# Output projection of both layers as seven block products, with the sums of its weight blocks made by adding transfers

## The chip, the cores and the metric

One NeuronCore of one Trainium2 chip runs the whole program. The metric is the device time of one execution in microseconds (us). The engines have short names in the profile: PE (TensorE, matrix products), DVE (VectorE), ACT (ScalarE), POOL (GpSimd), SP (SyncE, which here only issues transfers). PEld is the loading of weights into PE.

## What is computed

A decoder of two layers over 1024 tokens of 1024 features, all in float32. The lines that matter here:

```python
o_a = dilated_mixture(...)            # window attention, three groups of heads
o_b = stick_breaking_attention(...)   # the "stick attention"
gates = sigmoid(gate_pre + b_gate[l])
g_a, g_b = gates[..., :D_MODEL], gates[..., D_MODEL:]
merged = g_a * (o_a @ w_br[l, :OUT_A]) + g_b * (o_b @ w_br[l, OUT_A:])
x = x + merged @ w_o[l]               # the output projection
h2 = rmsnorm(x, norm2[l])
up = h2 @ w_up[l]
a, v = up[..., :D_FF], up[..., D_FF:]
a = causal_depthwise_conv(a, conv_w[l], conv_b[l])
x = x + (gelu(a) * v) @ w_down[l]
```

The change concerns `merged @ w_o`, a product of two 1024 x 1024 matrices, once in each layer, and what stands just before and behind it.

## The kernel before

**Arithmetic.** Every float32 operand of a product is split in two: a high part (rounded by ACT with a copy) and a low part (the rest, by a DVE subtraction); `split` does both. One product of a 128x128 weight tile with 512 tokens is then three matmuls: high x high, high x low, low x high. Features lie on partitions, tokens on columns; the 1024 tokens are two halves `n` of 512, the 1024 features eight chunks `e` of 128.

**Order.** The program is written as Python generators that are stepped in turn. The order of PE's instructions is the written order. The other engines' orders come from a scheduler that uses priorities, except in the part of the feed-forward behind its second unit, where they are also the written order. Each engine runs its instructions strictly in its order: one that waits holds all behind it.

**A layer, in order.** (1) The input projection runs in the background of the attention: the class `Dense` hands PE pieces of it (`share` counts them) between the pieces of the stick attention, then of the window attention. In the stick attention POOL masks the diagonal block of every score tile (`affine_select` on `beta`). (2) The branch stage: sixteen pairs `(n, e)` in the order of `todo`. For each pair PE makes two products `br_ps` (one for each branch), DVE multiplies each with its gate (`gin`, the gates being loaded three pairs ahead and put through a sigmoid by ACT), DVE adds both (`mrg`), ACT makes the high part `hh` and POOL the low part `hl` by a subtraction. All eight accumulator banks are used in turn. (3) The output projection: `wo_chunk` for each half `n` and chunk `e` of output features loads the 1024 x 128 weights, splits them in two pieces (ACT and DVE), accumulates 8 x 3 matmuls in `o_ps`; DVE adds the result to the residual `x`; ACT squares it and DVE sums the squares for the norm. That is 16 chunks of 24 matmuls in each layer. (4) The norm of half 0 runs beside the second half of the projection, the norm of half 1 beside the first products of the feed-forward. (5) The feed-forward: two plain units (`u_ps`, up_plain), then twenty units `up(j)` of seven block products each (`u_a`, `u_c`, `u_b`), which need sums of blocks of the normed input. Four of these sums (`S[3]`) are made in `first_sum`, under the output projection, the others in `sums`, under the two plain units. In the units `up(j)` POOL already issues one adding transfer each: `up_a` += `up_a` within on-chip memory.

**Lines that the steps touch.** `split` 141, `weights` 160, `product` 177, `drive` 189, `first_sum` 531, `norm` 540, `seven` 1049, `wo_chunk` 1316, `merged` 1417, the loop of the branch stage 1433 to 1466, the end of `mixer` 1467 to 1477, `sums` 1628, `up` 1643.

Of the kernel before, what the change touches and what calls it, by code (L numbers as in the profile page):

```python
# [32 lines left out]
NRAW = 2  # L33
PT = 6
# [25 lines left out]
def f32(ap):  # L60
    return ap.bitcast(F32)
# [3 lines left out]
def trunk_kernel(ctx, tc, x, xt, head0, norm1, vecs, w_in, w_br, w_o, w_up, w_down, norm_f, out, depth=None, probe=None):  # L65
# [59 lines left out]
    dn = [dr.tile([4, T], F32, name=f"dn{i}") for i in range(2)]  # L125
    fd = dr.tile([4, T], F32, name="fd")
# [31 lines left out]


# [62 lines left out]
    class Dense:  # L222
# [4 lines left out]
        def __init__(self):  # L227
            self.main, self.plain, self.seven, self.done = [], [], [], set()
            self.side, self.later, self.hooks = [], {}, []
            self.now = self.nxt = None  # L230
# [252 lines left out]
    def norm_add(n, e, first=False):  # L483

        if first:
            ACC[n] = sb.tile([P, HF], F32, tag="ql", bufs=2, name="nrm")
# [829 lines left out]
    def wo_chunk(l, n, e):  # L1316
        w = weights(w_o[l][:, e * P : (e + 1) * P], P)
        yield
        o = bank("ps", "o_ps")
        yield from product(o, [(w[k], h_part(n, k)) for k in range(KD)])  # L1320
        dve.tensor_tensor(xc(n, e), xc(n, e), o, ALU.add)
        norm_add(n, e, e == 0)
        yield

    def mixer(l, pending):
        R.clear()
        dense = Dense()
        gates = [pair_gate(dense, l, e) for e in range(KD)]
# [36 lines left out]
        attend(dense, items)  # L1365
        oh = {}
# [49 lines left out]

        def merged(n, e, m):
            act.copy(H[n][0][:, e, :], m)
            pool.tensor_tensor(H[n][1][:, e, :], m, f32(H[n][0][:, e, :]), ALU.subtract)

        wo = [wo_chunk(l, n, e) for n in range(2) for e in range(KD)]
# [14 lines left out]
        for i, ab in order:  # L1436
            n, e = todo[i]
            sl = slice(n * HF, (n + 1) * HF)
            if i not in seen:
# [4 lines left out]
                if i in X_AT:  # L1444
                    late_x = X_AT.index(i)
                    x_in(l, late_x // 2, late_x % 2)
# [11 lines left out]
            m = small("mrg")  # L1458
            dve.tensor_tensor(m, gt[:, 0, :], gt[:, 1, :], ALU.add)
            late.append((n, e, m))  # L1460
# [5 lines left out]
            if i == 12:  # L1466
                next(wo[0])
# [4 lines left out]
        def first_half():  # L1472
            yield from norm(0, g2[:, 0, :], "t", keep=True)
            yield from first_sum()

        drive(first_half(), relay(*wo, primed=True), 2.5, 36)
        return norm(1, g2[:, 0, :], "t", AF.Gelu, True)

    def ffn(l, pending, final):
# [125 lines left out]
        def up_plain(j, order, turns, extra):  # L1605
# [3 lines left out]
            w = [up_weights(j, 0), up_weights(j, 1)]  # L1609
# [18 lines left out]
        def sums():  # L1628

            new_s(1)  # L1630
# [713 lines left out]
```

## Time and profile before

| | |
|---|---|
| median of the runs | 2591.91 us (2591.76 to 2598.05, 3 runs) |
| the profiled execution's own time | 2593.59 us |
| its span | 2591.8 us |
| PE busy | 2577.4 us, 12536 instructions |
| DVE busy | 2061.1 us |
| ACT busy | 1334.1 us |
| POOL busy | 130.0 us |
| granted clock of PE | 1.00 |

The profile is one execution. "Busy" is the time in which an engine works on an instruction; matmuls overlap, so a busy PE can still be a PE that takes longer between two matmuls than it has to. A row of a group gives line, engine, operation, names (out<-in), shapes, count, then busy time and mean duration of one, then the idle time just before them and what ended it. A row of the timeline gives start, duration, engine, line, names and, in brackets, the idle time before it and its releaser. A row of windows gives for a stretch of time each engine's busy time (and its instructions), PE's granted clock, the busy share of the 16 transfer engines and GB/s.

### The profile page before, as it was taken

The numbers are of one execution on the slowest core, as the hardware profiler recorded it, in microseconds if no ns is written. First come the engines' busy times: TensorE is split into PE (matmuls) and PEld (weight loads), VectorE is DVE, ScalarE is ACT, GpSimd is POOL, SyncE is SP. The second block draws the span as 40 slices with busy tenths as digits, with TensorE's granted clock in tenths as the row PEclk, the third lists the DMA queues.
The fourth block names the chain that finished last, engine by engine and source line by source line (L and its number), as shares of the span: only waits on it lengthen the run. The fifth ranks groups of instructions, "written<-read, shape, count | busy, mean of one in ns | idle before, by whom it ended". The sixth has DMA issues, their size and how long they took to land.

```text
span 2591.8 us, 35872 instructions
## 1 busy us (share of the span) xinstructions
PE 2577.4 (99%) x12536; PEld 2153.4 (83%) x12536; DVE 2061.1 (80%) x3410; ACT 1334.1 (51%) x2488; POOL 130.0 (5%) x175
## 2 busy tenths in 40 slices
PE   9999999999999999999999999999999999999999
PEld 8888888888888888888888888888888888888887
DVE  8878877796878878897677788778868888879966
ACT  6555566664554545432445555666645555544223
POOL 1000000030000000000000000000300000000000
PEclk9999999999999999999999999999999999999999
DMA  7434579863355455688344436798634455457963
GB/s 261 152 114 145 158 197 233 235 224 105 103 158 166 155 186 155 246 323 312 147 149 147 127 129 188 199 242 235 198 99 129 138 174 164 157 184 251 347 241 134
DMA packets 402579, 480.02 MB, mean 185 GB/s; under 512 B 25272, under 2 KB 311392, under 8 KB 400736
## 3 DMA queue, kind: packets, MB, share of 16 engines
q1 hardware_dynamic: 395776, 464.85, 56.0%
q0 software_dynamic: 6464, 12.62, 2.7%
q8 instruction: 99, 1.62, 0.3%
q14 instruction: 80, 0.66, 0.1%
q10 hardware_dynamic: 160, 0.27, 0.0%
HBM read 308.74 MB, written 158.43 MB: 180 GB/s over the span
## 4 chain that ended last, share of the span: by engine, by line
PE 92%; DVE 4%; ACT 2%; DMA 1%; issue 1%; POOL 0%; DVEq 0%; ACTq 0%; POOLq 0%
PE u_a L1053 5%; PE u_a L1052 5%; PE u_a L1054 5%; PE d_ps L1801 5%; PE d_ps L1802 5%; PE d_ps L1803 5%; PE i_a L1052 5%; PE i_a L1053 5%; PE i_a L1054 5%; PE u_c L1052 3%; PE u_c L1053 3%; PE u_c L1054 3%; PE i_c L1052 2%; PE i_c L1054 2%; PE i_c L1053 2%; PE o_ps L182 2%
## 5 line engine op out<-in xcount | busy, mean ns | idle before, releaser
L144 ACT CAST w_hi<-up_a 128x512 fp32r<-128x512 f32 x280 | 174.4, 624 | 265.1 <-DVE up_a L1658 133.4
L152 DVE TENSOR_TENSOR w_lo<-up_a,w_hi 128x512 fp32r<-128x512 f32 x280 | 189.4, 688 | 64.4 <-ACT w_hi L144 64.2
L144 ACT CAST w_hi<-in_a 128x512 fp32r<-128x512 f32 x252 | 156.2, 622 | 157.7 <-PE i_c L1053 33.6
L152 DVE TENSOR_TENSOR w_lo<-in_a,w_hi 128x512 fp32r<-128x512 f32 x252 | 173.1, 689 | 72.3 <-ACT w_hi L144 60.7
L1812 DVE TENSOR_TENSOR x<-x,d_ps 128x512 f32<-128x512 f32 x220 | 150.5, 685 | 59.5 <-PE d_ps L1803 56.3
L1052 PE MATMUL u_a<-hh,w_hi 128*128 128x512 f32 x320 | 124.5, 389 | 0.0
L1053 PE MATMUL u_a<-hl,w_hi 128*128 128x512 f32 x320 | 124.5, 389 | 0.0
L1054 PE MATMUL u_a<-hh,w_lo 128*128 128x512 f32 x320 | 124.5, 389 | 0.0
L1052 PE MATMUL u_a<-t_hi,w_hi 128*128 128x512 f32 x320 | 124.5, 389 | 0.0
L1053 PE MATMUL u_a<-t_lo,w_hi 128*128 128x512 f32 x320 | 124.5, 389 | 0.0
L1054 PE MATMUL u_a<-t_hi,w_lo 128*128 128x512 f32 x320 | 124.5, 389 | 0.0
L1801 PE MATMUL d_ps<-gd_in,w_hi 128*128 128x512 f32 x316 | 123.2, 390 | 0.0
L1802 PE MATMUL d_ps<-gd_in,w_hi 128*128 128x512 f32 x316 | 123.0, 389 | 0.0
L1803 PE MATMUL d_ps<-gd_in,w_lo 128*128 128x512 f32 x316 | 123.0, 389 | 0.0
L1052 PE MATMUL i_a<-hh,w_hi 128*128 128x512 f32 x288 | 117.8, 409 | 0.0
L1052 PE MATMUL i_a<-t_hi,w_hi 128*128 128x512 f32 x288 | 116.4, 404 | 0.0
L1054 PE MATMUL i_a<-t_hi,w_lo 128*128 128x512 f32 x288 | 113.0, 392 | 0.0
L1054 PE MATMUL i_a<-hh,w_lo 128*128 128x512 f32 x288 | 113.0, 392 | 0.0
L1053 PE MATMUL i_a<-hl,w_hi 128*128 128x512 f32 x288 | 112.9, 392 | 0.0
L1053 PE MATMUL i_a<-t_lo,w_hi 128*128 128x512 f32 x288 | 112.9, 392 | 0.0
L1801 PE MATMUL d_ps<-gd_in,wd 128*128 128x512 f32 x284 | 110.8, 390 | 0.0
L1803 PE MATMUL d_ps<-gd_in,wd 128*128 128x512 f32 x284 | 110.5, 389 | 0.0
(422 smaller groups left out, 7695.3 us busy)
## 6 DMA issues: line engine op xcount, KB each, us to landing
gd<-g SPq DMA_DIRECT2D x154, 512.0 KB, 3.4
gd_in<-gd SPq DMA_DIRECT2D x154, 512.0 KB, 6.2
up_a<-in_w_up_dram SPq DMA_DIRECT2D x80, 512.0 KB, 5.4
in_a<-in_w_in_dram SPq DMA_DIRECT2D x72, 512.0 KB, 5.4
wd_raw<-in_w_down_dram SPq DMA_DIRECT2D x22, 1024.0 KB, 9.5
gin<-gs SPq DMA_DIRECT2D x32, 512.0 KB, 4.5
w_raw<-in_w_o_dram SPq DMA_DIRECT2D x64, 256.0 KB, 2.9
gs<-u SPq DMA_DIRECT2D x48, 256.0 KB, 3.2
```

The lines of the kernel that those rows point to most:

```text
L144: one = act.copy(hi, src)
L152: two = dve.tensor_tensor(lo, src, f32(hi), ALU.subtract)
L182: pe.matmul(o, lh, rh, start=(first and i == 0), stop=False, skip_group_check=share)
L1052: pe.matmul(o, w[0][:, c], rh, start=(first and i == 0), stop=False, skip_group_check=True)
L1053: pe.matmul(o, w[0][:, c], rl, start=False, stop=False, skip_group_check=True)
L1054: pe.matmul(o, w[1][:, c], rh, start=False, stop=(last and i == 3), skip_group_check=True)
L1801: pe.matmul(o, wh[:, c], gh, start=(i == 0 and k in (0, 4, 5)), stop=False, skip_group_check=True)
L1802: pe.matmul(o, wh[:, c], gl, start=False, stop=False, skip_group_check=True)
L1803: pe.matmul(o, wl[:, c], gh, start=False, stop=(i == m - 1), skip_group_check=True)
L1812: dve.tensor_tensor(x, x, o, ALU.add)
```

## The change

The merged matrix and the weights are cut into 2 x 2 blocks: the weights by output half `f` and by even and odd chunks of 128 input features (`j`), the merged matrix by token half `n` and the same even and odd chunks. `out_proj` makes the product from seven block products (order 0, 4, 1, 2, 3, 5, 6), each of 4 output chunks x 4 input chunks x 3 matmuls, 336 in a layer where there were 384. That needs four sums of weight blocks and sums of blocks of the merged matrix.

- **Sums of weight blocks**: `prepare` runs in the stick attention, one step with each `share` behind the fourteenth: SP copies 16 blocks of the weights (256 KB each) to `wof` in the chip's main memory, then POOL issues 16 adding transfers into `wof`, one in four steps.
- **Splitting in the stage**: `out_proj` loads each product's weights and splits them one product ahead. For products 1 to 4 ACT and DVE do it as before; for products 0, 5 and 6 (`ADDING`) ACT makes the high part and its negative, and an adding transfer of POOL from main memory makes the low part of that (`split_on`).
- **Sums of the merged matrix**: `merge` keeps blocks of it in float32 (`keep`), with signs changed for some (a scalar-tensor operation in place of the addition); `added` makes the sums, some by DVE, some by adding transfers; `merged` splits the sums that are needed at once. Four of the sixteen POOL subtractions of a layer go to DVE. The sums of products 1 to 3 are split inside `out_proj` (`beside`).
- **Result**: products 0 to 3 accumulate in the same four banks, 5 and 6 in the same four; after each product DVE adds or subtracts each bank to or from `x`: 28 times in a layer where it was 16.
- **Around it**: loads of `x` come later (one in the branch stage, three in `out_proj`); the weights of the first feed-forward unit are loaded and split in `out_proj`; `first_sum` is gone from under the projection, its four sums are made in `sums`; the steps of the norms are placed differently, and `drive` at the start of the feed-forward takes 0.5 in place of 0.7 and 3 steps ahead in place of 2.

```diff
+PREP = 14
+GAP_SUM = 4
+ADDING = (0, 5, 6)
+ADD1 = 3
+LATER = 3
...
+    def split_on(hi, lo, raw, src):
+        act.copy(hi, raw)
+        act.mul(lo, f32(hi), -1.0)
+        nc.gpsimd.dma_start(lo, src.bitcast(F32R), accum_op=ALU.add)
...
             self.fetch()
+            if self.prep and self.count > PREP:
+                next(self.prep, None)
             return True
...
-    def wo_chunk(l, n, e):
-        w = weights(w_o[l][:, e * P : (e + 1) * P], P)
-        yield
-        o = bank("ps", "o_ps")
-        yield from product(o, [(w[k], h_part(n, k)) for k in range(KD)])
-        dve.tensor_tensor(xc(n, e), xc(n, e), o, ALU.add)
-        norm_add(n, e, e == 0)
-        yield
+    def prepare(l):
+        def behind(one):
+            tc.add_manual_dep(one.ins, LAST["hi"], NO_SYNC, reason="behind")
+        blocks = [blocks_of(l, i) for i in range(4)]
+        for s in range(4):
+            for i in range(4):
+                behind(nc.sync.dma_start(wof[s, i], blocks[i][(2, 0, 0, 1)[s]]))
+                yield
+        for s in (0, 2, 1, 3):
+            for i in range(4):
+                src = wof[1 if s == 3 else 0, i] if s % 2 else blocks[i][3 if s == 0 else 2]
+                how = dict(max_dma_last_dim=4 * HF) if s % 2 else {}
+                behind(nc.gpsimd.dma_start(wof[s, i], src, accum_op=ALU.add, **how))
+                for _ in range(GAP_SUM):
+                    yield
+
+    def out_proj(l, keep, added):
+        order = (0, 4, 1, 2, 3, 5, 6)
+        into = ((0, 0), (1, 0), (1, 1), (0, 1), (0, 0), (1, 1), (1, 0))
...
+        def two(k, *some):
+            if k not in ws:
+                ws[k] = place(k)
+            for i in some:
+                if k in ADDING:
+                    split_on(*ws[k][i], raws[k][i], source(k)[:, i, :])
+                else:
+                    split(*ws[k][i], raws[k][i])
...
+        def beside(k, e):
+            c11, c12, c21 = keep[0, 0], keep[1, 0], keep[0, 1]
+            def one(i):
+                hi, lo = sums[1][i]
+                act.mul(hi, c11[:, i, :], -1.0)
+                dve.scalar_tensor_tensor(lo, c11[:, i, :], -1.0, f32(hi), ALU.mult, ALU.subtract)
+            if k == 0:
+                if e == 0:
+                    new_sum(1)
+                two(4, e)
+                if e % 2:
+                    load(1, e // 2)
+                if e < 3:
+                    one(e)
+                if e == 1:
+                    added(0, 0, 3)
...
+            elif k == 4:
+                if e == 0:
+                    one(3)
+                    new_sum(2)
+                two(1, e)
+                split(*sums[2][e], c12[:, e, :])
...
+        for at, k in enumerate(order):
+            if k == 0:
+                banks[0] = banks[1] = banks[2] = banks[3] = [bank("to"[e // 2], "o_ps") for e in range(4)]
+            elif k in (4, 5):
+                banks[k] = banks[6] = [bank(("ps", "s")[e // 2], "o_ps") for e in range(4)]
+            for e in range(4):
+                o, c = banks[k][e], slice(e * P, (e + 1) * P)
+                for i in range(4):
+                    (wh, wl), (gh, gl) = ws[k][i], part(k, i)
+                    pe.matmul(o, wh[:, c], gh, start=(i == 0 and k in (0, 4, 5)), stop=False, skip_group_check=True)
+                    pe.matmul(o, wh[:, c], gl, start=False, stop=False, skip_group_check=True)
+                    pe.matmul(o, wl[:, c], gh, start=False, stop=(i == 3), skip_group_check=True)
+                    if i == 1:
+                        yield
+                n, f = into[k]
+                x = xc(n, 4 * f + e)
+                with tc.high_priority(offset=AHEAD):
+                    dve.tensor_tensor(x, x, o, ALU.add if f or k == 4 else ALU.subtract)
+                beside(k, e)
+                yield
...
+        def added(n, j, p):
+            if j == 0:
+                c = keep[0, 0][:, p, :]
+                dve.tensor_tensor(c, c, keep[1, 0][:, p, :], ALU.add)
+            else:
+                nc.gpsimd.dma_start(keep[0, 1][:, p, :], keep[0, 0][:, p, :], accum_op=ALU.add)
...
         def merged(n, e, m):
-            act.copy(H[n][0][:, e, :], m)
-            pool.tensor_tensor(H[n][1][:, e, :], m, f32(H[n][0][:, e, :]), ALU.subtract)
+            hi, lo = H[n][0][:, e, :], H[n][1][:, e, :]
+            if n and e % 2 == 0:
+                t = small("mrg")
+                dve.tensor_tensor(t, m, keep[0, 0][:, e // 2, :], ALU.add)
+                split(hi, lo, t)
+                return
+            act.copy(hi, m)
+            pool.tensor_tensor(lo, m, f32(hi), ALU.subtract)
+            if n:
+                nc.gpsimd.dma_start(keep[1, 0][:, e // 2, :], m, accum_op=ALU.add)
...
+            if i % 4 == ADD1 and i > 4:
+                added(0, 0, i // 4 - 1)
+            if i % 4 == 0 and i > 4:
+                added(0, 1, i // 4 - 2)
+            if i == 10:
+                wo = out_proj(l, keep, added)
+            if i in (10, 12, 14):
+                next(wo)
...
-        drive(first_half(), relay(*wo, primed=True), 2.5, 36)
+        side = norm(0, g2[:, 0, :], "t", keep=True)
+        for n in (43, 0, 0, 1, 1):
+            for _ in range(n):
+                next(wo)
+            next(side)
+        drive(side, wo, 1.0)
+        early["lead"] = LATER
...
         def sums():
+            new_s(3)
             new_s(1)
             new_s(2)
             for i in range(4):
                 b11, b12, b21, b22 = B[1, i], B[0, i], B[1, 4 + i], B[0, 4 + i]
+                s3 = small("s3")
+                dve.tensor_tensor(s3, b22, b12, ALU.subtract)
+                split(*S[3][i], s3)
```

**How it moves instructions.** On DVE, at the seam from the branch stage to the output projection of the first layer. Names: `gin` the last gate products, `mrg` a merged chunk, `w_lo` and `wo_in` low parts of weights, `x` the residual, `m_part` the kept blocks, `m_hi` and `m_lo` their two parts. Before, from the last `gin` on:

```order
L1454 TENSOR_TENSOR gin<-gin,br_ps 128x512 [waits PE_49,Activation_49]
L1459 TENSOR_TENSOR mrg<-gin 128x512 [waits DVE_49,Pool_49]
L152 TENSOR_TENSOR w_lo<-w_raw,w_hi 128x512 [waits DMAHW1_49,PE_49,Activation_49]
L1321 TENSOR_TENSOR x_5858<-x_5858,o_ps 128x512 [waits PE_49]
L152 TENSOR_TENSOR w_lo<-w_raw,w_hi 128x512 [waits DMAHW2_49,Activation_49]
```

Now, from the same `gin` to the fourth split of the second product's weights:

```order
L1656 TENSOR_TENSOR gin<-gin,br_ps 128x512 [waits PE_49]
L158 TENSOR_TENSOR wo_in<-wo_raw,wo_in 128x512 [waits Activation_49]
L1602 SCALAR_TENSOR_TENSOR mrg<-gin 128x512 [waits DVE_49]
L1618 TENSOR_TENSOR mrg<-m_part 128x512
L1491 TENSOR_TENSOR x_5971<-x_5971,o_ps 128x512 [waits PE_49]
L1411 SCALAR_TENSOR_TENSOR m_lo<-m_part,m_hi 128x512 [waits Activation_49]
L158 TENSOR_TENSOR hl_5829<-mrg,hh_5828 128x512 [waits Activation_49]
L158 TENSOR_TENSOR wo_in<-wo_raw,wo_in 128x512 [waits DMAHW5_49]
L1411 SCALAR_TENSOR_TENSOR m_lo<-m_part,m_hi 128x512
L1491 TENSOR_TENSOR x_5971<-x_5971,o_ps 128x512 [waits PE_49]
L1610 TENSOR_TENSOR m_part<-m_part 128x512 [waits DMASW7_49,Pool_49]
L158 TENSOR_TENSOR wo_in<-wo_raw,wo_in 128x512
```

Eleven rows now stand behind the last gate product up to the last weights that the second block product needs; one of them waits for an adding transfer (DMASW). From the first gate product of the stage to the last there are 63 rows, before 56.

On DVE, in the first layer, where the two plain feed-forward units end and `up(2)` begins. Names: `up_a` its weights, `cv` the convolution's tiles, `u_ps` the plain units' accumulators. Before:

```order
L152 TENSOR_TENSOR w_lo<-up_a,w_hi 128x512 [waits DMAHW4_49,PE_49]
L1521 SCALAR_TENSOR_TENSOR cv<-u_ps,vec,cv 128x511 [waits Activation_49]
L1526 SCALAR_TENSOR_TENSOR cv<-halo,vec,cv 128x1
L1522 SCALAR_TENSOR_TENSOR cv<-u_ps,vec,cv 128x510 [waits DVE_49]
L1527 SCALAR_TENSOR_TENSOR cv<-halo,vec,cv 128x2 [waits DVE_49]
L152 TENSOR_TENSOR w_lo<-up_a,w_hi 128x512 [waits DMAHW5_49,DMASW5_49,PE_49]
```

Now:

```order
L1742 TENSOR_TENSOR cv<-cv,u_ps 128x512 [waits PE_49,Activation_49]
L158 TENSOR_TENSOR t_lo<-b_f_6769,t_hi 128x512 [waits Activation_49]
L1852 TENSOR_TENSOR b_f_6815<-b_f_6972,b_f_6769 128x512
L158 TENSOR_TENSOR g<-cv,g 128x512 [waits DMAHW0_49,Activation_49]
L158 TENSOR_TENSOR w_lo<-up_a,w_hi 128x512 [waits DMAHW2_49]
L158 TENSOR_TENSOR w_lo<-up_a,w_hi 128x512 [waits DMAHW3_49,DMASW1_49]
```

The first low part of `up(2)`'s weights stood ahead of the instruction that waits for the last plain product (`cv<-cv,u_ps`); now it stands four rows behind the start of that one.

More of the change, by code (lines that the diff above doesn't have):

```diff
@@ L1457, in mixer @@
                 continue
[L1458 to L1460 removed]
+            late.append(merge(i, gt))
             if len(late) > 1:
```

113 lines of the change are left out of this document (99 added, 14 removed).

## The prediction

> **What bounds the kernel now.** I read the page first: which engine is busy, and which work forms the chain that ended last.
>
> ```profile
> span 2591.8 us, 35872 instructions
> PE 2577.4 (99%) x12536; PEld 2153.4 (83%) x12536; DVE 2061.1 (80%) x3410; ACT 1334.1 (51%) x2488; POOL 130.0 (5%) x175
> DVE  8878877796878878897677788778868888879966
> PE 92%; DVE 4%; ACT 2%; DMA 1%; issue 1%; POOL 0%; DVEq 0%; ACTq 0%; POOLq 0%
> ```
>
> PE is the bound: nearly all of the span and of the chain. A matmul that goes is time that goes, unless another engine is then late. DVE is the candidate: it stands at eight tenths or more in most slices. So next PE's timeline, for the pace of its matmuls and its waits at both ends of the stage that is changed.
>
> ```profile
> 570.21 0.39 PE L182 MATMUL o_ps<-hh,w_hi 128*128 128x512 f32 x1
> 574.74 0.39 PE L184 MATMUL o_ps<-hh,w_lo 128*128 128x512 f32 x1
> 575.91 0.50 PE L183 MATMUL o_ps<-hl,w_hi 128*128 128x512 f32 x1 [0.55 <-POOL hl L1419]
> 623.21 0.95 PE L546 MATMUL nrm_t<-ones,nrm 128*128 128x1 f32 x8
> 624.02 0.49 PE L182 MATMUL o_ps<-hh,w_hi 128*128 128x512 f32 x1
> 713.97 0.50 PE L1052 MATMUL u_c<-hh,w_hi 128*128 128x512 f32 x1 [0.57 <-ACT u L1674]
> 1998.15 0.50 PE L1052 MATMUL u_c<-hh,w_hi 128*128 128x512 f32 x1 [0.99 <-ACT u L1674]
> ```
>
> The first row is the first matmul of the output projection; the second comes 20 matmuls later, so the pace is 4.53/20 = 0.2265 us. Last I read the windows of three stages in both layers: first to last gate product (`gin`), the output projection, and the two plain feed-forward units.
>
> ```profile
> core 0: us, PE busy (x) PEld busy (x) DVE busy (x) ACT busy (x) POOL busy (x), PEclk, DMA share, GB/s
> 531.27:577.59 46.32, 45.77 (x202) 37.60 (x201) 43.83 (x57) 31.77 (x53) 19.81 (x15) 1.00 0.70 228
> 570.21:659.99 89.78, 89.04 (x397) 73.20 (x396) 59.09 (x88) 38.52 (x65) 5.32 (x5) 1.00 0.32 93
> 659.99:705.08 45.09, 45.09 (x206) 37.24 (x204) 43.07 (x75) 24.93 (x42) 1.80 (x2) 1.00 0.38 105
> 1816.00:1861.35 45.35, 45.35 (x202) 37.55 (x201) 43.43 (x57) 31.86 (x53) 20.33 (x15) 1.00 0.70 233
> 1854.94:1943.76 88.82, 88.75 (x398) 73.28 (x397) 58.26 (x87) 38.16 (x64) 5.18 (x4) 1.00 0.31 91
> 1943.76:1988.84 45.08, 45.08 (x205) 37.24 (x204) 42.38 (x74) 25.01 (x42) 1.78 (x2) 1.00 0.37 104
> ```
>
> The output projection has room on every other engine (DVE 59.09 of 89.78), but its neighbours have none on DVE: 43.83 of 46.32 and 43.07 of 45.09. The clock is full throughout. 384 matmuls take 86.98 by the pace; the first layer's 2.80 above that are about 1.2 for the norm's small products (0.81 from `nrm_t` to the next matmul, the rest an estimate for its broadcast) and 1.6 of waiting, the second layer's 1.84 the same 1.2 and 0.6.
>
> **The change part by part.** *Matmuls removed.* 48 in each layer, 96 x 0.2265 = **-21.7 us**, all on PE's path.
>
> *The seam into the output projection.* DVE finishes the gate products behind PE: PE starts the projection at 570.21 and 1854.94, DVE ends the last `gin` at 577.59 and 1861.35 (the windows' ends). What DVE has to do there, by these groups and rows:
>
> ```profile
> L1454 DVE TENSOR_TENSOR gin<-gin,br_ps 128x512 f32<-128x512 f32 x64 | 41.8, 679 | 2.0 <-ACT gin L1399 2.0
> L1459 DVE TENSOR_TENSOR mrg<-gin 128x512 f32<-128x512 f32 x32 | 32.6, 1018 | 2.4
> L152 DVE TENSOR_TENSOR br_w<-br_raw,br_w 128x512 fp32r<-128x512 f32 x16 | 13.0, 815 | 0.1
> L152 DVE TENSOR_TENSOR w_lo<-w_raw,w_hi 128x512 fp32r<-128x512 f32 x80 | 61.4, 771 | 35.4 <-ACT w_hi L144 35.1
> L152 DVE TENSOR_TENSOR g<-cv,g 128x512 fp32r<-128x512 f32 x154 | 105.7, 687 | 1.4 <-ACT g L144 1.4
> L1419 POOL TENSOR_TENSOR hl<-mrg,hh 128x512 fp32r<-128x512 f32 x32 | 44.4, 1392 | 170.3 <-ACT hh L1418 105.9 <-PE br_ps L184 64.4
> 705.35 0.69 DVE L1534 TENSOR_TENSOR cv<-cv,u_ps 128x512 f32<-128x512 f32 x1 [0.20 <-PE u_ps L184]
> 705.95 0.68 DVE L152 TENSOR_TENSOR w_lo<-up_a,w_hi 128x512 fp32r<-128x512 f32 x1
> ```
>
> The last two rows start 0.60 apart, though each lasts 0.69: a row of DVE costs 0.60. A POOL subtraction costs DVE too: the groups that run beside it are longer than the 687 of a plain subtraction, by 331 (`mrg`), 128 (`br_w`) and 84 (`w_raw`); (331x32 + 128x16 + 84x80)/32 = 0.60 us for each of the 32. From first to last `gin` there are now 63 DVE rows for 56: +4.2; four POOL subtractions fewer in each layer: -2.4. The last `gin` moves by +1.8, to 579.4 and 1863.15. Then eleven rows stand before the fourth split of the second product's weights, as the first pair of orders above shows: 6.6, and 1.2 for two POOL subtractions still running, so 587.2 and 1870.95. PE wants that low part 59 matmuls after its start (48 of the first product, 11 of the second): 583.6 and 1868.3. It waits 3.6 and 2.6.
>
> One of the eleven rows waits for an adding transfer, and so do three like it in the stage.
>
> ```profile
> L1651 POOL DMA_DIRECT2D up_a<-up_a x40 | 35.1, 878 | 905.1 <-DVE up_a L1661 235.3 <-DVE up_a L1658 180.0 <-DVE hl L566 178.7
> L723 POOL TENSOR_SCALAR_AFFINE_SELECT beta<-beta 128x128 f32<-128x128 f32 x64 | 31.4, 490 | 530.7 <-ACT beta L717 449.6 <-DMA in_a<-in_w_in_dram 42.0 <-DVE w_lo L152 28.8
> up_a<-up_a POOLq DMA_DIRECT2D x40, 256.0 KB, 3.3
> fx<-fd POOLq DMA_DIRECT2D x8, 256.0 KB, 7.5
> ```
>
> Two of the waiting rows stand 8 rows behind the `mrg` whose sum they take, the other two 13. From `mrg` to the landing go 0.69 for itself, some 1.1 until POOL is free and issues, and the transfer. Landing in 3.3, as the same kind within on-chip memory does, it is there about when DVE comes (8 rows at 0.60 to 0.67 are 4.8 to 5.4): I take 1.0 a layer, from 0 to 8.7 (the 7.5 of `fx`, worked out below). Behind DVE's wait stand the accumulator's addition to `x`, the fourth split, and so PE. Waits 4.6 and 3.6, less the 1.6 and 0.6 of now: **+3.0 and +3.0**.
>
> *Inside the projection.* DVE adds to `x` 28 times for 16, splits kept blocks and weights; with the first two products it has about 4.5 rows in every 2.72 us (12 matmuls), all that it can do; from the third on, splits stand a product (10.9 us) ahead. Loads of 256 to 1024 KB are asked for one product ahead and land in 3 to 8. ACT gets some 25 more copies at 0.62, 15 beside its 38.52. I take 0, and 2 a layer as the upper end. The norm's steps come closer, 6 matmuls (1.36 us) from `nrm_t` to its broadcast, where the root and reciprocal end about 1.46 after `nrm_t` starts (the reciprocal below): 0 to 0.5 each, I take 0.
>
> ```profile
> 624.49 0.18 DVE L549 RECIPROCAL ss<-ss 128x4 f32<-128x4 f32 x1
> 700.48 0.69 DVE L152 TENSOR_TENSOR w_lo<-up_a,w_hi 128x512 fp32r<-128x512 f32 x1
> 706.55 1.29 DVE L1539 TENSOR_TENSOR cv<-cv 128x512 f32<-128x512 f32 x2
> ```
>
> *Start of the feed-forward.* Four more subtractions and four more splits (`s3`) go into the stretch where DVE has 2 us left: 8 x 0.60 = 4.8. By the second pair of orders the first low part of `up(2)`, now at 700.48, stands four rows behind the `cv` that starts at 705.35, on the last plain product: at 705.35 + 4 x 0.60 = 707.75, ended 708.4. PE wants it two matmuls into `up(2)`, at 705.53: it waits 2.9. The lag is now paid at the second `u_c`, 0.57 and 0.99, which I let go with it: **+2.3 and +1.9**.
>
> *Stick attention.* POOL gets 16 issues a layer at 0.88, beside 32 masks at 0.49; 130.0 us busy of the span is the cover for POOL itself, and the copies find transfer engines that are half idle. I take 0. If some 11 masks a layer stood right behind an issue and PE waited for each, it would be 2 x 11 x 0.88 = 19.
>
> Sum: -21.7 + 6.0 + 4.2 = **-11.5**. The profiled execution's own time is 2593.59 (span 2591.8 and 1.8 around it): 2582.1. It lies 1.68 above the median: **2580.5**.
>
> **The rivals.** *Full gain.* The lag of DVE doesn't reach PE: the two neighbours' spare 2 us and a pace below 0.60 take it up. Against it speak both windows; for it, that PE's waits now are under 2 us in places as tight. Some 2.5 of waiting stay: -19, 2573. Chance 0.15.
>
> *Late adding transfers, the other side.* If they land as `fx` does (7.5), the row 8 behind waits 7.5 + 1.8 - 5.4 = 3.9, the second, with more rows of POOL's beside it, 3.0, the two 13 behind 0.9 each: 8.7 a layer where I took 1.0. -11.5 + 2 x 7.7 = +3.9: 2595.8, slower than before. It decides from a landing of about 7.0 us (3.4 + 2.5 + 0.4 + 0.4 = 6.7 a layer). For it: the stage's transfer engines are at 0.70, where `up_a` runs at 0.38. Against: these stay on chip, as `up_a` does. Chance 0.18.
>
> *Masks behind issues.* A quarter of the 19 above: +5, 2585.5. The masks wait for ACT, 449.6 us in all, so POOL is usually there first. Chance 0.12.
>
> *POOL can't issue while DVE works.* The stage gets twelve issues a layer (eight for sums, four for the first product's weights), where DVE leaves (46.32 - 43.83)/46.32 = 5.4% free; were an issue to run in that alone, 0.88 would become 16 us, and twelve of them 195: less the 46 us of the stage, some 150 a layer, 2880. Two issues between 659.99 and 705.08, DVE busy for 43.07 of 45.09, took 1.80 together, and all 40 have a mean of 878: chance 0.02. The Trainium skill has this rule ("SBUF — State Buffer", section "SBUF: two separate sides"): a GpSimd-issued transfer's descriptors can't be written while VectorE holds the port that both share, and the page gives 620 ns alone and some 3100 beside a copy. By its 3100, an estimate, the 24 issues of both layers would cost up to 24 x 2.2 = 53 more; the trace doesn't show it with subtractions on DVE.
>
> **How the numbers follow.** Forecast 0.53, rivals 0.15, 0.18, 0.12, 0.02. The forecast's own range is 2576 to 2587: 2 a layer inside the projection upward, the waits at both seams halved downward. The range goes from 2572, at the edge of the full gain, to 2595, short of the late transfers' value, which leaves out something under 2 in 10. A difference of 0.3%, 7.8 us, is about what a measurement of this kernel can tell from none: faster means below 2584.1, slower above 2599.7. Faster: 0.15, three quarters of the forecast and little else, 0.55. Slower: the last rival and the late transfers where they come with a term at its upper end, 0.08. The same: 0.37.
>
> **What would show it.** The projection's stretch should shrink from 89.8 to about 82, with one wait of 3 to 5 us on PE near 583, ended by a low part from DVE, and one of 2 to 3 at the start of `up(2)`. Wrong would be: PE without either (full gain); DVE idle for 2 us and more ahead of the sums of kept blocks, ended by a transfer; masks that start later than ACT ends; issues far over 0.9 us. That DVE's last `gin` doesn't come later would break the first step of the seam.

## The result and the profile after

The changed kernel takes 2627.66 us (median of 4, 2625.81 to 2630.62), the kernel before 2592.11 in the same series: ratio 1.0133, 95% interval 1.0115 to 1.0150. It is slower by 35.5 us, where 11.5 us of gain were forecast. The profiled execution's own time is 2630.62, 37.0 more than that of before. The first rows of its page and its chain:

```profile
span 2628.9 us, 35747 instructions
PE 2575.4 (98%) x12440; PEld 2146.3 (82%) x12440; DVE 2073.7 (79%) x3450; ACT 1353.7 (51%) x2528; POOL 182.3 (7%) x239
PE 68%; DMA 4%; DVE 4%; ACT 2%; issue 1%; POOL 0%; DVEq 0%; ACTq 0%; SPq 0%; POOLq 0%
```

The 96 matmuls are gone (12536 to 12440). The chain could be followed back only to 535 us, so its shares add up to 79%, and PE's 68% can't be set beside the 92% of before; of the part that was followed, transfers have 4 of 79, where they had 1 of 100. PE's busy time has hardly fallen, although it has 21.7 us less to do: a matmul takes longer in places. The windows show where. Columns are as before. The first three rows are the output projection, the plain units and the first 22 us of the third unit in the first layer; the next two are the projection and the plain units of the second layer; the last two are short stretches of the first projection.

```profile
571.58:672.86 101.28, 86.40 (x349) 68.99 (x348) 64.37 (x102) 47.25 (x82) 16.89 (x18) 0.90 0.61 161
672.86:717.75 44.89, 44.89 (x206) 37.33 (x204) 40.12 (x71) 24.44 (x41) 0.89 (x1) 1.00 0.19 53
717.75:740.00 22.25, 18.67 (x74) 14.63 (x73) 18.62 (x31) 10.24 (x19) 0.00 (x0) 0.92 0.44 166
1877.52:1976.57 99.05, 85.80 (x349) 68.67 (x348) 63.23 (x100) 47.20 (x82) 17.68 (x18) 0.91 0.61 164
1976.57:2021.46 44.89, 44.89 (x205) 37.32 (x204) 40.20 (x71) 24.48 (x41) 0.88 (x1) 1.00 0.19 53
577.91:582.64 4.73, 4.29 (x9) 2.96 (x10) 1.32 (x3) 0.00 (x0) 0.00 (x0) 0.51 0.46 92
650.26:657.67 7.41, 7.41 (x23) 6.26 (x24) 3.29 (x6) 2.58 (x5) 0.89 (x1) 0.50 0.65 173
```

The projection takes 101.28 us where it took 89.78, and 99.05 for 88.82, with 48 matmuls fewer. Its 336 matmuls and small products need 76.1 + 1.2; it loses 24.0 and 21.8, where before it lost 1.6 and 0.6. The granted clock is the second thing to see: 0.90 over the projection, a half in the two short windows. In the trace of before it is 1.00 in every one of these stages. PE's timeline has the waits, and the pace behind them:

```profile
577.91 0.80 PE L1485 MATMUL o_ps<-hh,wo_in 128*128 128x512 f32 x1 [4.35 <-DMA wo_in<-in_w_o_dram]
578.50 0.63 PE L1483 MATMUL o_ps<-hh,wo_in 128*128 128x512 f32 x1
578.93 0.63 PE L1484 MATMUL o_ps<-hl,wo_in 128*128 128x512 f32 x1
579.99 0.79 PE L1485 MATMUL o_ps<-hh,wo_in 128*128 128x512 f32 x1 [0.43 <-DMA wo_in<-in_w_o_dram]
592.95 0.50 PE L1485 MATMUL o_ps<-hh,wo_in 128*128 128x512 f32 x1 [0.73 <-DVE wo_in L158]
595.35 0.50 PE L1485 MATMUL o_ps<-hh,wo_in 128*128 128x512 f32 x1 [1.44 <-DVE wo_in L158]
650.26 1.87 PE L561 MATMUL nrm_t<-ones,nrm 128*128 128x1 f32 x8 [7.86 <-DVE nrm L506]
721.17 0.50 PE L1069 MATMUL u_a<-hh,w_lo 128*128 128x512 f32 x1 [2.81 <-DVE w_lo L158]
```

Five waits in the first projection, 14.8 us together: two for low parts of the first product's weights, which an adding transfer brings; two in the second product for low parts from DVE; one of 7.86 in front of the norm's product. Behind each long wait matmuls start 0.43 apart, not 0.2265 (578.50 to 578.93). The other 9 us of the 24.0 are put down to that pace and to the slower first matmuls behind each wait; they are a difference, not a measurement. The last row is the forecast wait at the third feed-forward unit.

Stage by stage, the 37.0 us are: branch stages +0.6 and +2.5 (first and second layer), projections +11.5 and +10.2, plain units -0.2 and -0.2, the first 240 matmuls of the third unit on +4.9 and +4.4, and 3.4 in all the rest (most of it in the stick attention, see below).

What stood behind the waits on the other engines, by their timelines (first DVE, with one row of the second layer, and ACT; then POOL, again with one row of the second layer):

```profile
568.47 0.69 DVE L1602 SCALAR_TENSOR_TENSOR mrg<-gin 128x512 f32<-128x512 f32 x1
581.32 0.69 DVE L1610 TENSOR_TENSOR m_part<-m_part 128x512 f32<-128x512 f32 x1 [7.83 <-DMA m_part<-mrg]
1886.82 0.69 DVE L1610 TENSOR_TENSOR m_part<-m_part 128x512 f32<-128x512 f32 x1 [8.44 <-DMA m_part<-mrg]
645.67 0.62 ACT L150 CAST w_hi<-w_raw 128x512 fp32r<-128x512 f32 x1 [3.78 <-DMA w_raw<-in_w_up_dram]
646.20 0.62 ACT L504 ACTIVATE sq<-x 128x512 f32<-128x512 f32 x1
```

```profile
568.90 0.88 POOL L170 DMA_DIRECT2D wo_in<-in_w_o_dram  x1 [0.76 <-ACT wo_in L169]
570.84 0.88 POOL L170 DMA_DIRECT2D wo_in<-in_w_o_dram  x1 [1.06 <-ACT gin L1572]
573.84 0.88 POOL L1624 DMA_DIRECT2D m_part<-mrg  x1 [2.12 <-DVE gin L1656]
1880.37 0.89 POOL L1624 DMA_DIRECT2D m_part<-mrg  x1 [1.59 <-issue]
```

DVE stood still for 7.83 us at one sum, for a transfer issued at 573.84, with the last gate products in its queue. That transfer adds the `mrg` that DVE had begun at 568.47: its issue came 5.4 us later, behind two issues of the first product's low parts that had waited for ACT (568.90 and 570.84) and a wait of its own, and it landed 7.4 after that. In the second layer the same two stretches are 7.0 (from 1873.36) and 6.4. PE's wait ended at 577.87 with the landing of the transfer issued at 568.90, 9.0 us later. ACT made a high part of feed-forward weights at 645.67, when their load had come, and only then a square that the norm waits for. The table of issues gives the landings, which had been the disputed number:

```profile
up_a<-up_a POOLq DMA_DIRECT2D x40, 256.0 KB, 3.3
m_part<-mrg POOLq DMA_DIRECT2D x8, 256.0 KB, 6.8
m_part<-m_part POOLq DMA_DIRECT2D x8, 256.0 KB, 5.7
wo_in<-in_w_o_dram POOLq DMA_DIRECT2D x8, 256.0 KB, 7.2
```

All four have one size. The first runs in the feed-forward, the other three in the branch stage and at the start of the projection, where single ones land in 3.3 to 9.1. Within one kind the landing goes with the share of the transfer engines between issue and landing: `m_part<-m_part` took 3.3 at 0.45 (issued at 582.67), 5.5 at 0.59 (595.34) and 8.3 at 1.02 (1871.79). The issue itself takes 0.88 to 0.91 in the median, about as before.

### The profile page after: what moved, and what is told of

Read it like the earlier page. It is cut to its first block, busy times and chain, and to the rows that moved or that the text cites. A ratio compares the mean times of both kernels' runs of the same rounds, so it can differ in the third digit from the quotient of the medians.

```text
span 2628.9 us, 35747 instructions
## 1 busy us (share of the span) xinstructions
PE 2575.4 (98%) x12440; PEld 2146.3 (82%) x12440; DVE 2073.7 (79%) x3450; ACT 1353.7 (51%) x2528; POOL 182.3 (7%) x239
## 4 chain that ended last, share of the span: by engine, by line
PE 68%; DMA 4%; DVE 4%; ACT 2%; issue 1%; POOL 0%; DVEq 0%; ACTq 0%; SPq 0%; POOLq 0%
PE u_a L1069 6%; PE u_a L1068 5%; PE u_a L1067 5%; PE d_ps L2013 5%; PE d_ps L2015 5%; PE d_ps L2014 5%; PE u_c L1067 3%; PE u_c L1068 3%; PE u_c L1069 3%; PE i_a L1067 2%; PE i_a L1068 2%; PE i_a L1069 2%; PE u_b L1068 1%; PE u_b L1069 1%; PE u_b L1067 1%
```

## Experiments

Two theories stood at first. **Late transfers**: PE and DVE wait for adding transfers that land late in the full branch stage. **DVE's rows**: the forecast's mechanism, only larger. A third was added for the norm (ACT behind loads) and a fourth for the slow matmuls (the clock falls behind an idle stretch). Edits are to the changed kernel unless said otherwise; "2628" in an expectation is that kernel.

**The first product's weights from DVE, the sums from DVE, both, and later loads.**

```diff
-ADDING = (0, 5, 6)
+ADDING = (5, 6)
```

> The first product's weights get their low parts from DVE again (four subtractions a layer in the branch stage) and no longer from adding transfers. Late transfers as the cause: PE's wait of 4.4 us for the low part of the first product goes in both layers, DVE's wait of 7.8 for a sum of the merged matrix stays, so the second product is still late: the seam's loss of about 12 us falls to about 8 in each layer, 2619 us. DVE's load as the cause: four more rows at 0.60, nothing else moves: 2632.

```diff
-                nc.gpsimd.dma_start(keep[0, 1][:, p, :], keep[0, 0][:, p, :], accum_op=ALU.add)
+                dve.tensor_tensor(keep[0, 1][:, p, :], keep[0, 1][:, p, :], keep[0, 0][:, p, :], ALU.add)
...
-                nc.gpsimd.dma_start(keep[1, 0][:, e // 2, :], m, accum_op=ALU.add)
+                dve.tensor_tensor(keep[1, 0][:, e // 2, :], keep[1, 0][:, e // 2, :], m, ALU.add)
```

> The eight adding transfers a layer that make sums of the merged matrix become eight DVE additions; the first product keeps its adding transfers. Late transfers as the cause: DVE's wait of 7.8 us goes, PE's wait for the first product's low parts stays at 4 to 5 and the half clock behind it; the eight rows cost DVE 4.8: the seam's loss falls from 12 to about 8, 2619 us. DVE's load as the cause: +4.8 a layer, 2637.

The third kernel has both edits.

> Both: no adding transfer in the branch stage, twelve more DVE rows in each layer. Late transfers as the cause: no wait of PE or DVE for a transfer at the seam; what stays is DVE's row count, 12 x 0.60 = 7.2 us more than the forecast's 3.6, so a loss of 8 to 11 where it is 12: 2620 to 2627, with no half clock if it comes in waits under a microsecond. DVE's load as the cause: the loss grows by 7.2 to about 19 a layer: 2642.

In the fourth the loop that takes the weights of the first plain unit (`early["up"]`) stands under product 5 and not under product 3.

> The weights of the first plain feed-forward unit are loaded and split one product later (beside the sixth product, not the fifth). ACT behind loads as the cause of PE's 8 us in front of the norm's product: the squares no longer stand behind four splits that wait for their loads, the 8 us and some 2 us of half clock behind them go in both layers: 2607 us, less 1 to 3 if the first plain unit then waits. The lag from the seam as the cause: the 8 us stay, 2628.

Measured: 2614.54 (ratio to before 1.0086, 1.0071 to 1.0101), 2620.84 (1.0108), 2626.20 (1.0126) and 2626.72 (1.0131). The first two are faster by 13 and 7 although each gives DVE more rows, so transfers do cost; both together give almost nothing, as the count of rows had it. In the first one DVE never waits over 0.5 us from 555 to 596, and PE waits for DVE instead:

```profile
555.44 0.69 DVE L158 TENSOR_TENSOR wo_in<-wo_raw,wo_in 128x512 fp32r<-128x512 f32 x1 [0.16 <-ACT wo_in L150]
595.96 0.69 DVE L158 TENSOR_TENSOR wo_in<-wo_raw,wo_in 128x512 fp32r<-128x512 f32 x1 [0.42 <-ACT wo_in L150]
565.23 0.50 PE L196 MATMUL br_ps<-oh_a,br_w 128*128 128x512 f32 x1 [3.31 <-DVE br_w L158]
641.84 1.87 PE L561 MATMUL nrm_t<-ones,nrm 128*128 128x1 f32 x8 [5.05 <-DVE nrm L506]
```

The first two are DVE's only waits there. Without late transfers DVE's pace is the bound, at the branch weights now. By the last row the norm's wait fell too, from 7.86 to 5.05, so not all of the 13 us was lost at the seam. (No trace shows the waits of the second kernel.) The fourth says nothing of its theory: the scheduler gave ACT's copies and SP's loads the places they had.

**Order on ACT, late sums, both, and DVE's rows at the third unit.** Here the order is forced with a dependency within the engine (`LAST` holds the latest square, on ACT, and the latest sum of squares, on DVE; the high and the low parts of the weights are put behind them):

```diff
-                    early["up"].append(weights(w_up[l][:, (e - 2) * DFF : (e - 2) * DFF + P], P))
+                if e == 3:
+                    put = LAST["sq"], LAST["na"]
+                    early["up"] = [weights(w_up[l][:, v * DFF : v * DFF + P], P, behind=put) for v in range(2)]
```

> On ACT the four squares of the last product of half 0 are made to stand ahead of the four high parts of the first feed-forward weights, which stood between them; nothing is left out or added. ACT behind loads as the cause of PE's 8 us in front of the norm's product: the 8 us and some 2.5 us of half clock behind them go in both layers, -20 in all: 2608 us. The lag from the seam as the cause: PE still waits 5 us and more there, 2625 or above.

```diff
-            if i % 4 == ADD1 and i > 4:
+            if i % 4 == ADD1 and 4 < i < 15:
...
                 if e == 1:
-                    added(0, 0, 3)
+                    added(0, 0, 2)
...
                 if e == 3:
+                    added(0, 0, 3)
```

> The last two sums that DVE makes of the merged matrix, the ones that wait for an adding transfer, go later: one from the branch stage into the first product, one two steps back. Late transfers as the cause, with both consumers: DVE's wait of 7.8 us shrinks to under 2, PE's wait of 4.4 for the first product's low parts stays, so the second product's waits of 0.9 and 1.6 go and the clock behind them: -3 to -5 a layer, 2618 to 2622 us. The first product's transfers alone as the cause: no change, 2628.

> Both of the foregoing. If they are separate causes, the gains add up: about 2600 us. If one lag is behind both, the result is that of the better one alone, 2608.

```diff
-                s3 = small("s3")
-                dve.tensor_tensor(s3, b22, b12, ALU.subtract)
-                split(*S[3][i], s3)
```

> The eight DVE rows and four ACT copies a layer that make the fourth sums at the start of the feed-forward are left out; the seventh block products read another sum in their place. DVE's rows as the cause of PE's 3 us at the start of the third unit: the low part of its weights stands ahead of the last plain product's instruction again, the 3 us and the half clock behind them (1.5) go in both layers, 2619 us, with 0.6 to 1 us left at the second product of that unit as before. Transfers or loads as the cause: no change, 2628.

Measured: 2614.47 (1.0086, 1.0071 to 1.0101), 2625.51 (1.0131), 2610.99 (1.0070), 2617.84 (1.0098). With the squares first the norm's wait falls from 7.86 to this row, and in the second layer PE doesn't wait there:

```profile
643.61 1.05 PE L561 MATMUL nrm_t<-ones,nrm 128*128 128x1 f32 x8 [1.57 <-DVE nrm L506]
```

That is 13 of the 20 us expected, and it settles the norm: steps for four pieces of weights that stood ahead of four squares and their sums. The edit moves the copies on ACT and the subtractions on DVE together and doesn't tell the two apart. Late sums changed nothing: DVE met the moved row at the same time and still waited 7.48 us, since the scheduler had set it among the last gate products again; so the third kernel, with both edits, is close to the first alone. Leaving the fourth sums out (the result is then another) took PE's 2.8 us away, and the first 240 matmuls from there took 55.27 us, as before the change; -10 as DVE's rows had it, though four ACT copies a layer went with them.

**Weights sooner and sums later by force; fewer rows by transfers; all; a filled wait.** In the first, the second half of the first product's weights is loaded into `acc`, and the two last sums get a dependency on the addition to `x`.

> Only the branch stage and the first product are touched, with no more DVE rows. The second half of the first product's weights is loaded into the norm's accumulator, which is free then, and so some 13 us sooner; the last two sums that DVE makes of the merged matrix are made to stand behind the additions to the residual in the first product. Late transfers as the cause, with PE and DVE both waiting: no wait of over 1 us for a transfer at the seam in either engine; what stays is DVE's pace, up to the forecast's 3.6 us, so the loss of 10 to 12 at the seam falls to about 4, -6 to -8 in each layer: 2612 to 2616 us. DVE's rows as the cause: the same rows, the same time, 2628.

```diff
-                split(*S[2][i], b12)
+                split_on(*S[2][i], b12, b12)
```

(and the same for `S[3]`)

> At the start of the feed-forward the low parts of the second and fourth sums come from adding transfers (ACT makes the negative of the high part) and not from DVE: eight DVE rows a layer fewer, all work done. DVE's rows as the cause of PE's 3 us at the third unit: as where the fourth sum was left out, -10 us, 2618. If the transfers bring a new wait there, 2625 and above.

> The edits of the squares first, of early weights and late sums, and of low parts by adding transfers together. If the three are separate causes, their gains add up: 2628 - 13 - 14 - 10 = 2591 us, some us less if the shorter waits leave the clock at full speed (less 4 to 8): 2583 to 2591. If a lag moves from one place to the next, 2600 and above.

```diff
         tot = bank(tag, "nrm_t")
+        if keep and n == 0:
+            filler = H[1][0]
+            for _ in range(34):
+                pe.matmul(tot, filler[:, 0, 0:P], filler[:, 0, :], start=True, stop=True, skip_group_check=True)
```

> 34 matmuls whose result nothing reads (7.7 us at full speed) are put in front of the norm's product of half 0, where PE waits 8 us in each layer; the wait and all else stay. Clock lowered by idling as the cause of the matmuls of 0.43 us behind the wait: these go, about 11 in each layer at 0.20 each and slower small products, -2.5 to -3.5 a layer: 2621 to 2623 us, faster with more work. A clock lowered by something else: 2628 to 2629.

Measured: 2624.67 (1.0120), 2624.96 (1.0124), 2610.72 (1.0068, 1.0055 to 1.0080), 2621.02 (1.0110, 1.0096 to 1.0123). In the first, DVE's wait of 7.8 is gone, PE's is not: ACT's steps kept their place, so the issue did (572.81), and it landed at 578.91.

```profile
578.95 0.51 PE L1487 MATMUL o_ps<-hh,wo_in 128*128 128x512 f32 x1 [3.19 <-DMA wo_in<-in_w_o_dram]
```

Low parts by adding transfers moved the wait at the third unit from its first product to its second, where ACT is late; in front of that ACT had waited 1.25 for one of those transfers (722.02) and 1.63 for DVE (728.12):

```profile
729.80 0.50 PE L1067 MATMUL u_c<-hh,w_hi 128*128 128x512 f32 x1 [3.58 <-ACT u L1886]
```

All together gain 17, not 37: two of the three mends had mostly moved a lag. The filled wait is the clearest of all: with 68 matmuls of no use the kernel is 6.6 us faster by the medians, and by the two traces the stretch from the last matmul in front of the wait to the first plain unit is shorter by 3.3 and 3.7 us in the two layers.

```profile
640.14 7.87 PE L563 MATMUL nrm_t<-hh 128*128 128x512 f32 x34
648.23 1.05 PE L565 MATMUL nrm_t<-ones,nrm 128*128 128x1 f32 x8 [0.23 <-DVE nrm L506]
649.47 0.40 PE L1488 MATMUL o_ps<-hl,wo_in 128*128 128x512 f32 x1
649.71 0.40 PE L1489 MATMUL o_ps<-hh,wo_in 128*128 128x512 f32 x1
```

The norm's product waits as long as it did, but behind it matmuls start 0.24 apart and not 0.43. So the slow matmuls are the price of the idle stretch itself. In this trace the wait at the third unit is left, 2.8 in both layers, with no half clock behind it: not every wait of nearly 3 us costs one.

**What sets the seam, and a version with everything mended.** In the first, ACT's two steps for all four blocks go to gate pair 11, behind loads as above. In the second, the splits of `S[3]` move into the third unit. The third has the mends without new transfers (weights and ACT's steps for them sooner, sums late, squares first, the norm's step two half-chunks later, the splits moved); the fourth is the third with the first product's low parts from DVE, and with their loads and ACT's steps where they were.

> The first product's weights are loaded sooner as in the ninth run, and ACT's two steps for all four blocks stand four gate pairs sooner too, so that the adding transfers can be issued some 8 us earlier; the sums stay as they were. If PE's wait at the first product is a matter of the issue's time: it goes, DVE's wait of 7.8 for its sum stays and sets the second product: 2620 to 2623 us. If the transfers land late however early they are issued: PE still waits 3 and more there, 2627.

> The four splits of the fourth sums go from the start of the feed-forward into the third unit, four DVE rows and four ACT copies a layer; nothing is left out and no transfer is added. DVE's rows as the cause of the 3 us there: the low part of the third unit's weights stands ahead of the last plain product's instruction, the wait falls to under 1 us and the half clock goes: -8 to -10 us, 2618 to 2620. If the copies then hold ACT, a wait at the second product of that unit grows: 2624 and above.

> All mends without new transfers: first product's weights sooner with ACT's steps, late sums, the squares first with the feed-forward's weights behind them and the norm's step 2.7 us later, the four splits moved into the third unit; the low parts of the first product by adding transfers. If the lost time is in these places alone: seam loss 4 a layer, norm and third unit under 1 each, clock at full speed: 2628 - 13 - 16 - 10 - some 4 of clock = 2585, below the kernel before. If a lag only moves on: 2600 and above.

> As the foregoing, but the first product's low parts come from DVE, with loads where they were: four more DVE rows a layer, no transfer that PE waits for. If the landing decides at the seam: better than the foregoing or equal, 2583 to 2588. If DVE's pace decides: PE waits 3 to 4 us for the branch weights, as where this was done alone, and the time is 5 to 8 us above the foregoing: 2590 to 2595.

Measured: 2626.01 (1.0134), 2624.39 (1.0120), 2619.57 (1.0106, 1.0092 to 1.0120), 2598.09 (1.0019, 1.0010 to 1.0027). In the first, PE's wait at the first product goes, as the issue's time had it, and comes back 20 us sooner (DVE, then PE):

```profile
553.83 0.69 DVE L1610 TENSOR_TENSOR m_part<-m_part 128x512 f32<-128x512 f32 x1 [7.08 <-DMA m_part<-mrg]
558.17 0.80 PE L196 MATMUL br_ps<-oh_a,br_w 128*128 128x512 f32 x1 [7.80 <-DVE br_w L158]
```

POOL now issues two weight transfers (541.49, 542.13) right ahead of a sum's (543.98), which lands only at 553.74, 9.8 us later; DVE stands at that sum, and with it the branch weights for PE. The moved splits had the result of the transfers: 3.0 us more at the unit's second product. The pair at the end differs in the first product's weights alone, and is 21 us better with their low parts from DVE than from transfers issued sooner; in the third kernel PE waits for the branch weights again, 8.08 us at 558.20. The fourth kernel's windows, projection and branch stage of the first layer, and the longest wait that is left:

```profile
577.25:655.88 78.63, 77.76 (x350) 64.26 (x348) 58.57 (x94) 39.99 (x70) 13.71 (x14) 1.00 0.68 186
526.51:577.25 50.74, 46.37 (x194) 37.85 (x193) 48.91 (x66) 34.12 (x57) 19.05 (x15) 0.93 0.85 254
564.13 0.80 PE L196 MATMUL br_ps<-oh_a,br_w 128*128 128x512 f32 x1 [4.37 <-DVE br_w L158]
```

The projection takes 78.63 for the 77.3 it needs; the branch stage, 43.52 before, takes 50.74, with DVE at 48.91 of it. Over both layers, in this trace against that of before, the projections gain 11.2 and 10.2; the branch stages lose 7.2 and 7.4, the third units 3.9 and 3.5, the plain units some 0.9 each, and 3.8 are lost in the rest.

**Two more on that version.** The fourth sums back under the projection's end (with the norms' steps spaced); and on top of it the first two low parts from adding transfers again.

> The sixteenth run, but the fourth sums are made under the end of the projection again, as in the kernel before, and the norm's steps stand one or two steps further apart. If the loss at the third unit is DVE's and ACT's work there: its 3 us fall to about 1 and the half clock with it, -3 to -4 a layer, and -1 a layer at the small products: 2588 to 2591 us, below the kernel before. If the lag moves into the plain units: 2596 and above.

> The foregoing, with the first two of the four low parts of the first product's weights from adding transfers, two DVE rows a layer fewer. If DVE's pace alone decides at the seam: -1.2 a layer, 2 us below the foregoing. If the two transfers hold up others in POOL's queue: DVE or PE waits for a transfer again, 4 us and more above the foregoing.

Measured: 2599.61 (1.0030, 1.0021 to 1.0039) and 2606.95 (1.0048, 1.0035 to 1.0061). In the first the third unit runs at full pace (54.8 us for 240 matmuls), and the plain units, 44.89 in the changed kernel, take 52.3, with small waits for late parts of the norm:

```profile
662.00 1.02 PE L561 MATMUL nrm_t<-ones,nrm 128*128 128x1 f32 x8 [1.18 <-DVE nrm L506]
666.78 1.09 PE L570 MATMUL nrm_b<-ident,ss 128*128 128x128 f32 x4 [1.30 <-DVE ss L564]
```

The lag moved by one stage. In the second PE waits at the first product again (4.57 us longer between two matmuls), but not for an adding transfer:

```profile
577.39 0.50 PE L1483 MATMUL o_ps<-hh,wo_in 128*128 128x512 f32 x1 [4.41 <-ACT hh L1623]
573.75 1.33 ACT L1572 ACTIVATE gin<-gin,vec 128x512 f32<-128x512 f32 x2 [2.69 <-DMA gin<-gs]
```

It waits for a high part of the merged matrix, which ACT makes behind the sigmoid of the last gates, and the load of these gates, an ordinary transfer, had come late. DVE waits for no transfer there. Neither expectation has this wait, and whether the two adding transfers delayed the load is not shown. No version came below the kernel before.

## Why the prediction was wrong

- **Matmuls removed, -21.7.** Right: 12440 are left, and where nothing waits their pace is 0.2265.
- **The seam, +6.0 forecast.** Failed: the adding transfers were taken at 1.0 a layer for DVE and at nothing for PE.
  - *DVE's rows.* Their count held within about 1 us: without its wait of 7.83 the last gate product would have ended near 579.5 (it ended at 587.3), where 579.4 was forecast. That it comes so near is luck: DVE's first gate product came 0.75 later than before, and two more waits for transfers, 1.21 and 1.65, are in it.
  - *The transfers' price at DVE.* The 1.0 rested on a landing of 3.3 and an issue some 1.8 us behind the start of `mrg`; one DVE row alone waited 7.83 and 8.44. Of that the landing has 4.1 and 3.1 (7.4 and 6.4 in place of 3.3) and the late issue 3.6 and 5.2 (5.4 and 7.0 in place of 1.8). The second rival, with a chance of 0.18, had the landing right (7.5) but not the issue, and its 8.7 was spread over four rows; that the sums are so close is in part luck.
  - *PE's own wait.* A second consumer wasn't costed at all: PE itself needs the first product's low parts from such transfers, by way of SP, ACT and POOL in turn, and waited 4.35 and 3.15. The forecast wait in the second product (3.6 in the first layer) came as two of 0.73 and 1.44, PE being late itself by then.
  - *The misread row.* The landing of 3.3 was read off the feed-forward and set beside a share of 0.38, which holds for 2 of its 20 issues a layer; from 705 to 1060, where the other 18 of the first layer run, the share is 0.52 in the trace of before. The stage's own window, 0.70, stood beside it, and in the changed kernel it reads 1.04 between 570 and 580.
- **Inside the projection, 0 forecast.** Failed: 7.9 and 7.5 us in front of the norm's product. The step counted ACT's copies (15 us more, beside 38.52 of 89.78) and not their order: copies that wait for loads stood ahead of squares, and on DVE the subtractions behind them ahead of the sums. Shown by the fifth kernel.
- **Start of the feed-forward, +4.2 forecast.** Right in mechanism and wait (2.9 forecast; between two matmuls 2.97 more in both layers), shown by the eighth kernel. But the lag at the second product did not go with it, and half clock came on top: the first 240 matmuls took 4.9 and 4.4 longer than before.
- **The clock, not in the sum.** Failed: every price had been a wait, and each wait of 2.8 us and more in the changed kernel also cost a stretch at half clock, with the slower first matmuls some 9 us in the first projection. The twelfth kernel shows it for the norm's wait. The Trainium skill says so ("TensorE: Matmul & The Clock Gate", section "Why this matters for your kernels": no idle gaps of PE above some 3 us between bursts). The trace agrees for 4.35 and 7.86, and goes further: behind waits of 0.73 and 1.44 within 3 us the pace fell to 0.43 as well (from 596.17), in the first layer only.
- **Stick attention, 0 forecast.** Nearly right: in front of its products `z` PE waits 1.5 us in the first layer and 2.1 in the second, before 0.2 each, which is most of the 3.4 above. It waits for ACT's `stay` (1.24 at 135.23, 1.47 at 1439.22) and not for the third rival's masks on POOL.
- **POOL can't issue while DVE works.** Wrong as its chance said: an issue took 0.88. The first rival, the full gain, is out with the waits above.

The change loses in three ways: what was given to transfers to spare DVE came back as waits of DVE and PE, in a stage with its transfer engines at 0.70 before; ACT and DVE took weights in hand ahead of the norm; and the waits brought half clock. The mended kernel (2598.09) wins back most of that and is 5.6 us above the kernel before. What stays open: how much could be won by taking rows off DVE in the branch stages, where it still loses 7.2 and 7.4 with DVE busy for 48.91 of 50.74; no kernel here did that.

## What to carry to other kernels

A transfer that takes work off a full engine has a price where it is waited for: take its landing from a stage as loaded as the one it goes into, and follow every queue that it passes (load, cast, issue, consumer), since each runs in order. On an engine, idle time is no proof of room: ask what stands ahead of the instruction that someone waits for. And a wait of PE of some 3 us can cost more than its length.

## What the runs showed of the hardware

- Adding transfers of 256 KB land in 3.3 us (median; 4.4 at most) in the feed-forward, where the transfer engines are at 0.52 (705 to 1060), and in 5.7 to 7.2 (medians; 9.1 the longest) in the branch stage and at the start of the projection, where they are at 0.85 (531 to 588; 1.04 between 570 and 580); 9.8 in an experiment, behind two others. The issue takes POOL 0.88 to 0.91 in the median in both.
- In the changed kernel half clock came in stretches of 3.4, 6.8 or 10.2 us, part of them inside the wait: 5 or so us of slow matmuls behind a wait of 4.4, 7 behind one of 7.9. Useless matmuls in the longer wait removed the stretch behind it. A wait of 2.8 had such a stretch behind it in the changed kernel and none in that experiment.
- Matmuls that start 0.2265 apart at full clock start 0.43 apart at half.
